# A streaming encoder layer on one core: part of the weights split ahead of the second phase, its first rows brought in piece by piece, and its first loads in another order

## The chip, the core and the metric

The kernel runs on one core of one Trainium2 chip. The time is the device time of one execution in microseconds (us); lower is better. A core has a matrix engine (TensorE, PE in the profile, with its weight loads as PEld), a vector engine (VectorE, DVE), an activation engine (ScalarE, ACT), GpSimd (POOL) and a sync engine (SyncE, SP) that here does nothing but issue DMA transfers. Each engine works through its own list of instructions in order; semaphores hold an instruction back until what it needs is there.

## What is computed

One layer of a hybrid streaming encoder over a prompt of 2048 tokens and a sample of 32 tokens (2080 columns together), model width 1024, float32 throughout:

```
h   = rmsnorm(x)
z   = h @ W_in          # 1024 -> 5376: q, k, v, four gates, conv input, two merge gates
A   : sliding-window attention, 8 heads on 2 kv heads, yA = (attn * silu(gA)) @ W_A
B   : gated causal convolution of width 3,             yB = (B * conv(C * u) * silu(gB)) @ W_B
r   = x + (sigmoid(mA) * yA + sigmoid(mB) * yB) @ W_o
out = r + sigmoid(r @ W_pg) * (p @ W_pp)
```

The keys, values and convolution rows that a next step needs are written out too.

## The kernel before

**Two halves of a float32.** TensorE multiplies in a rounded format (fp32r). To keep float32 accuracy, both operands are cut in two: `hi` is the rounded value (a copy on ACT), `lo = value - hi` the rest (a subtraction on DVE). Every product is then three matmuls, hi*hi, hi*lo and lo*hi. So each weight piece of 128x512 that comes from HBM costs one ACT copy and one DVE subtraction before TensorE can use it. The raw piece lies in one of 8 buffers tagged `wf`, the split piece in one of WB = 5 buffers of the pool `wp` (`w` in the profile); the split function is at L228, its two operations at L229 and L230.

**Fewer products by sums of quadrants.** The large products are done by a Strassen-like scheme: seven products p = 1 to 7 of quadrant combinations in place of eight. Of the weight operand, p = 1, 2 and 4 are plain quadrants, and p = 7, 5, 6 and 3 are sums of up to four quadrants (`WS`, L332).

**First phase (L1201 to L1230, first product at L611).** z = h @ W_in for all tokens, in groups g = 0 to 20 of output columns: first the token columns 0 to 1023 (steps named `(0, g, p)`), then the rest (`(1, g, p)`, and with a fourth element, a letter, where a second level of the scheme runs at L749). A hand-written list `steps` orders them. What comes out goes to DRAM: q, k, v, gates, the conv rows `z_y`, the tanh of the merge gates `z_t`. Beside this, after step `(0, g, 6)` for g = 1 to 8, `quad_sums` (L368) prepares the quadrant sums of W_o (UO) and W_pg (UPG) for the second phase: four raw loads of 256 KB on SP, four additions on DVE, four stores to the DRAM tiles `quad_sum` by GpSimd (L377). Its tiles come from the pool of 15 rows `tmp`. Near the end of the phase, after steps `(1, 20, 6)` and `(1, 20, 7)`, `conv_rows` (L855) loads and splits the first three of four token blocks of the conv rows (12 loads at L850, 12 splits at L233 and L234) that the second phase starts with.

**Second phase (all of it recorded at L158 of the profile).** Here the order of the instructions of every engine is written out by a planner in the kernel: it advances a clock of its own (`now`) by a modelled cost for every instruction (`cost_queue`, L119), keeps count of free buffers (`limit`, `live`), and emits each instruction when the model says that its inputs are there. Loads land 5.2 us after their issue in its model. TensorE's work is the list `plan` (L307): yB for the blocks 0 to 3, pp = p @ W_pp, yA of block 0 and 1, the 28 products of W_o and the 28 of W_pg for the first half of the tokens (`first`, `products_of`, L296), yA of block 2 and 3, and the 28 + 28 products of the second half. Between these, the attention of 17 token tiles is started at given points of TensorE's work (L2022): every 11 us for the first eight. An attention tile loads q (`zq`), k and v (`zkv`) and the rotary table (`cs`), transposes on TensorE and takes turns on ACT, DVE and GpSimd.

**Weights in the second phase.** `next_loads` (L1924) is called whenever nothing else is due. It first issues the row loads of the next units, then raw weight loads up to LOOK = 11 pieces ahead into the `wf` buffers, while SP is not more than 0.5 us booked, and then starts splits (`split_w`, L1910) in order as soon as one of the 5 `w` buffers is free. One product of W_o or W_pg uses one piece; so does one unit of yA.

```
while n_load[0] < min(len(worder), used[0] + LOOK) and busy["Y"] < now[0] + 0.5:
    ...
    if raw_key(key):
        uu, e = raw_key(key)
        eY.dma_start(out=t, in_=wu[uu, :, 4 * e:4 * e + 4, :])
    else:
        eY.dma_start(out=t, in_=quad_sum[key[2:4]][:, WS[key[4]]])
```

The functions that the change touches, with the line numbers of the profile:

## Time and profile before

| | |
|---|---|
| median of 3 runs | 1530.45 us (1529.68 to 1532.38) |
| the profiled execution | 1533.35 us |
| its span, first to last instruction | 1531.6 us |
| share of the span: ACT, GpSimd | 53%, 24% |
| moved by DMA | 346.89 MB, mean 226 GB/s |
| weight splits in the second phase (`w<-wr`, L158) | 168 on ACT, 168 on DVE |

In rows of stretches of time, an engine's busy time stands in us with the number of its instructions; PEclk is the clock that TensorE was granted (1.00 is full speed), and the DMA share is the mean busy share of the 16 DMA engines. A matmul's span in the trace overlaps with the next one's, so that "busy" for PE means that some matmul was under way; what is missing from the length of the stretch is time in which PE stood still. In rows of waits stand: the instruction that waited, what ended the wait, us in total, how often, the longest. In rows of groups: busy us and mean ns of one, then the idle time before. In rows of DMA issues: KB of one and the us from issue to landing.

### The profile page before, as it was taken

Reading aid. Unit: us, or ns where it says so; the run is one execution under the profiler, and the core shown is the slowest. Engines: PE = TensorE matmul, PEld = TensorE weight load, DVE = VectorE, ACT = ScalarE, POOL = GpSimd, SP = SyncE. Lnnn points to the kernel's source line nnn. Section 1 sums busy time; section 2 is a strip of 40 time slices with the busy share of each in tenths; the row PEclk is TensorE's granted clock in tenths of the full one; section 3 lists DMA queues with packets and bytes.
Section 4 is the critical chain, followed back from the end, with each engine's and each line's share of the span. In section 5 each row is a group of like instructions: output and inputs, shape, how many; then the busy total and the mean of one; then the engine's idle time right before and its main releaser. Section 6 shows DMA issues by size and latency. Waiting matters only on the chain.

```text
span 1531.6 us, 27944 instructions
## 1 busy us (share of the span) xinstructions
PE 1500.7 (98%) x9553; PEld 1355.8 (89%) x9553; DVE 1227.2 (80%) x2330; ACT 818.2 (53%) x1933; POOL 370.5 (24%) x534
## 2 busy tenths in 40 slices
PE   9999999999999999999999999999999999999998
PEld 7878888888889999999999889998877787999998
DVE  7896887875589776899965878868998899769777
ACT  8353354344467634434544546786766586544453
POOL 2133332332212222333222111103313213211201
PEclk9999999999999999999999999999999999999999
DMA  9479886898777845343556776658947749985959
GB/s 340 151 276 342 313 295 216 282 344 266 241 279 257 315 149 195 112 132 119 175 192 187 265 234 205 210 186 231 239 127 184 187 128 300 312 240 145 254 143 288
DMA packets 199231, 346.89 MB, mean 226 GB/s; under 512 B 23728, under 2 KB 57072, under 8 KB 199088
## 3 DMA queue, kind: packets, MB, share of 16 engines
q1 hardware_dynamic: 157008, 239.42, 48.4%
q0 software_dynamic: 32432, 87.85, 19.9%
q10 hardware_dynamic: 9648, 17.83, 3.1%
q8 instruction: 75, 1.23, 0.3%
q14 instruction: 68, 0.56, 0.1%
HBM read 227.66 MB, written 117.46 MB: 225 GB/s over the span
## 4 chain that ended last, share of the span: by engine, by line
PE 38%; DVE 7%; ACT 3%; DMA 2%; issue 2%; SPq 0%; ACTq 0%; DVEq 0%
PE b L158 17%; PE yB L158 5%; PE yA L158 5%; PE O L158 2%; PE S L158 2%; DVE c L158 1%; PE la L749 1%; PE pp L158 1%; PE a L611 1%; PE a L613 1%; PE a L616 1%; PE PT L158 1%; DVE w L158 1%; DVE xb_l L158 1%; DVE tk L158 1%
## 5 line engine op out<-in xcount | busy, mean ns | idle before, releaser
L158 PE MATMUL b<-xb_h,w 128*128 128x264 f32 (+1 forms) x1344 | 315.3, 326 | 7.2 <-DVE c L158 4.5
L158 PEld LDWEIGHTS b<-xb_h,w 128*128 128x128 f32 x1344 | 225.1, 190 | 27.6 <-DVE c L158 4.2
L613 PE MATMUL a<-x_l,w 128*128 128x264 f32 (+1 forms) x744 | 228.1, 320 | 0.0
L611 PE MATMUL a<-x_h,w 128*128 128x264 f32 (+1 forms) x744 | 227.1, 319 | 0.0
L158 PE MATMUL b<-xb_l,w 128*128 128x264 f32 (+1 forms) x672 | 218.4, 325 | 0.8 <-DVE xb_l L158 0.8
L616 PE MATMUL a<-x_h,w 128*128 128x264 f32 (+1 forms) x744 | 201.6, 320 | 0.0
L229 ACT CAST w<-wr 128x512 fp32r<-128x512 f32 (+1 forms) x180 | 110.2, 619 | 105.7 <-PE c L616 35.4
L230 DVE TENSOR_TENSOR w<-wr,w 128x512 fp32r<-128x512 f32 (+1 forms) x180 | 136.1, 767 | 33.9 <-ACT w L229 32.7
L158 ACT CAST w<-wr 128x512 fp32r<-128x512 f32 x168 | 103.5, 623 | 105.7 <-PE b L158 53.0
L611 PEld LDWEIGHTS a<-x_h,w 128*128 128x128 f32 x744 | 139.9, 188 | 10.5
L613 PEld LDWEIGHTS a<-x_l,w 128*128 128x128 f32 x744 | 139.7, 188 | 10.7
L158 PEld LDWEIGHTS b<-xb_l,w 128*128 128x128 f32 x672 | 127.8, 190 | 10.8 <-DVE xb_l L158 1.6
L616 PEld LDWEIGHTS a<-x_h,w 128*128 128x128 f32 x744 | 125.0, 188 | 10.7
L158 DVE TENSOR_TENSOR w<-wr,w 128x512 fp32r<-128x512 f32 x168 | 117.8, 706 | 14.1 <-ACT w L158 13.4
L749 PE MATMUL la<-x_h,w 128*128 128x264 f32 x516 | 112.2, 285 | 1.9 <-ACT w L229 1.2
L613 PE MATMUL c<-x_l,w 128*128 128x512 f32 (+1 forms) x336 | 110.7, 339 | 0.0
L611 PE MATMUL c<-x_h,w 128*128 128x512 f32 (+1 forms) x336 | 110.6, 340 | 0.0
L229 ACT CAST w<-a 128x512 fp32r<-128x512 f32 x82 | 49.7, 620 | 98.1 <-DVE a L360 31.5
L616 PE MATMUL c<-x_h,w 128*128 128x512 f32 (+1 forms) x336 | 100.4, 340 | 0.0
L810 DVE SCALAR_TENSOR_TENSOR u<-u,c 128x264 f32<-128x264 f32 (+1 forms) x125 | 59.4, 506 | 44.5 <-ACT u L805 30.0
L158 PE MATMUL yB<-ycs_h,w 128*128 128x264 f32 (+1 forms) x384 | 91.0, 326 | 0.0
L805 ACT COPY u<-a 128x264 f32<-128x264 f32 (+1 forms) x114 | 47.4, 437 | 80.7 <-PE a L616 80.7
(435 smaller groups left out, 3877.8 us busy)
## 6 DMA issues: line engine op xcount, KB each, us to landing
wr<-in_wu SPq DMA_DIRECT2D x177, 256.0 KB, 4.1
a<-in_wu SPq DMA_DIRECT2D x116, 256.0 KB, 5.3
wr<-ws SPq DMA_DIRECT2D x74, 256.0 KB, 3.5
wr<-qs SPq DMA_DIRECT2D x64, 256.0 KB, 3.9
ws<-a POOLq DMA_DIRECT2D x63, 256.0 KB, 4.0
qs<-a POOLq DMA_DIRECT2D x24, 256.0 KB, 5.8
z_s<-s2n POOLq DMA_DIRECT2D x21, 264.0 KB, 5.0
s<-z_s SPq DMA_DIRECT2D x21, 264.0 KB, 4.5
```

Source lines behind the costliest of these rows:

```text
L158: return f(**kw)
L229: nc.scalar.copy(out=hi, in_=src)
L230: nc.vector.tensor_tensor(out=lo, in0=src, in1=hi.bitcast(F32), op=sub)
L611: nc.tensor.matmul(out=ps[:, :cn], lhsT=w[:, 0, k], rhs=x[0][:, c0:c0 + cn], start=first and k == 0, stop=False, skip_group_check=True)
L613: nc.tensor.matmul(out=ps[:, :cn], lhsT=w[:, 0, k], rhs=x[1][:, c0:c0 + cn], start=False, stop=False, skip_group_check=True)
L616: nc.tensor.matmul(out=ps[:, :cn], lhsT=w[:, 1, k], rhs=x[0][:, c0:c0 + cn], start=False, stop=k == 3, skip_group_check=True)
L749: nc.tensor.matmul(out=ps[:, :m], lhsT=w[:, a, k], rhs=r[:, cols], start=q in "ABG" and j == 0 and e == 0, stop=j == 1 and e == 2, skip_gr ...
L805: nc.scalar.copy(out=t[:, c0:c0 + cn], in_=ps[:, :cn])
L810: nc.vector.scalar_tensor_tensor(out=t[:, c0:c0 + cn], in0=t[:, c0:c0 + cn], scalar=-1.0, in1=ps[:, :cn], op0=mul, op1=sub)
```

## The change

Six things are done at once.

1. For the 16 quadrant sums of W_o (p = 7, 5, 6, 3 for n = 0 to 3), `quad_sums` now also splits the sums, and stores hi and lo, 512 KB in place of 256 KB (`store_split`). The sums of W_pg are stored raw as before.
2. The 8 raw pieces of W_A, which yA uses (`piece_split`), are loaded in the first phase, split, and stored as hi and lo in `wa_split`.
3. In the second phase, pieces that are stored split (`stored`) skip the raw load and the split: one DMA of 512 KB goes straight into a `w` buffer when one is free. Each of the 8 pieces of W_A is used in each of four blocks, each of the 16 sums in two halves, which makes 64 such loads in place of 64 raw loads with their 64 ACT copies and 64 DVE subtractions.
4. The loads of the sums and pieces come at steps `(0, g, 6)`, their arithmetic at `(0, g, 7)`, a few products later; W_o at g = 1, 3, 5, 7, W_pg at g = 9, 11, 13, 15, the pieces of W_A at g = 2, 4, ... 16. Their tiles come from a pool of five of their own (`zpool`) and not from `tmp`.
5. The conv rows of blocks 0, 1 and 2 are loaded earlier than they are split: loads after the steps `(1, 20, 1)`, `(1, 20, 6)` and `(1, 19, 5)`, splits after `(1, 20, 6)`, `(1, 19, 5)`, and for block 2 one row at a time in the last set of products.
6. In the second phase, the second attention tile starts at 6 us of TensorE's work and not at 11, and no raw weight is loaded before the planner's clock has passed 8 us.

```diff
--- before.py
+++ after.py
@@ -363,18 +363,45 @@
         for p, i in WS.items():
             nc.gpsimd.dma_start(out=wsum[g][:, i], in_=sums[g][p])
 
-    quad_sum = {(x, n): dram.tile([P, 4, 4, P], F32, tag=f"qs{x}_{n}", name=f"qs{x}_{n}") for x in (UO, UPG) for n in range(4)}
+    quad_sum = {(x, n): dram.tile([P, 4, 1 + (x == UO), 4 * P], F32, tag=f"qs{x}_{n}", name=f"qs{x}_{n}")
+                for x in (UO, UPG) for n in range(4)}
+    wa_split = [dram.tile([P, 2, 4 * P], F32, tag=f"wa{n}", name=f"wa{n}") for n in range(8)]
+
+    def quad_load(name, u, e):
+        t = zp.tile([P, 4 * P], F32, tag="z", name=name)
+        nc.sync.dma_start(out=t.rearrange("p (a b) -> p a b", a=4), in_=wu[u, :, 4 * e:4 * e + 4, :])
+        return t
+
+    def store_split(dst, t, name):
+        h = tmp(f"h{name}", F32R)[:, :512]
+        split(h, t.bitcast(F32R), t)
+        nc.gpsimd.dma_start(out=dst[:, 0], in_=h.bitcast(F32))
+        nc.gpsimd.dma_start(out=dst[:, 1], in_=t)
 
     def quad_sums(x, n):
-        t = {}
-        for name, u, e in (("a11", n, 0), ("a21", n + 4, 0), ("a22", n + 4, 1), ("a12", n, 1)):
-            t[name] = tmp(f"{name}_{x}_{n}")[:, :512].rearrange("p (a b) -> p a b", a=4)
-            nc.sync.dma_start(out=t[name], in_=wu[x + u, :, 4 * e:4 * e + 4, :])
-        t["sc"] = tmp(f"sc_{x}_{n}")[:, :512].rearrange("p (a b) -> p a b", a=4)
+        t = {name: quad_load(f"{name}_{x}_{n}", x + u, e)
+             for name, u, e in (("a11", n, 0), ("a21", n + 4, 0), ("a22", n + 4, 1), ("a12", n, 1))}
+        yield
+        t["sc"] = zp.tile([P, 4 * P], F32, tag="z", name=f"sc_{x}_{n}")
         for o, v, w in (("sc", "a11", "a21"), ("a21", "a21", "a22"), ("a11", "a11", "a21"), ("a12", "a12", "a11")):
             nc.vector.tensor_tensor(out=t[o], in0=t[v], in1=t[w], op=add)
         for p, o in ((7, "sc"), (5, "a21"), (6, "a11"), (3, "a12")):
-            nc.gpsimd.dma_start(out=quad_sum[x, n][:, WS[p]], in_=t[o])
+            if x == UO:
+                store_split(quad_sum[x, n][:, WS[p]], t[o], f"{p}_{x}_{n}")
+            else:
+                nc.gpsimd.dma_start(out=quad_sum[x, n][:, WS[p], 0], in_=t[o])
+
+    def piece_split(n):
+        t = quad_load(f"wa_{n}", UY + n, 0)
+        yield
+        store_split(wa_split[n], t, f"wa_{n}")
+
+    def stored(key):
+        if key[0] == "q" and key[3] == 0:
+            return wa_split[key[2] - UY]
+        if key[0] == "B" and key[2] == UO and key[4] in WS:
+            return quad_sum[key[2:4]][:, WS[key[4]]]
+        return None
 
     def raw_key(key):
         if key[0] == "q":
@@ -852,12 +879,16 @@
 
     yc = {}
 
-    def conv_rows(b):
+    conv_in = {}
+
+    def conv_load(b):
+        conv_in.update({(b, c): load_row(f"yc{b}_{c}", z_y[c], b) for c in range(4)})
+
+    def conv_split(b, cs=range(4)):
         nt = blk(b)[1]
-        for c in range(4):
-            t = load_row(f"yc{b}_{c}", z_y[c], b)
+        for c in cs:
             yc[b, c] = pair(f"ycs{b}_{c}")
-            split_half(yc[b, c][0][:, :nt], yc[b, c][1][:, :nt], t[:, :nt])
+            split_half(yc[b, c][0][:, :nt], yc[b, c][1][:, :nt], conv_in.pop((b, c))[:, :nt])
 
 
 
@@ -1198,7 +1229,15 @@
         refills[at_step[at_]] = p
     after = {at_step[1, pairs_[9], 2, "C"]: sets[0]}
     after.update({at_step[1, sets[i - 1][-1], 5]: sets[i] for i in range(1, len(sets))})
-    sums_at = {(0, 1 + 2 * n + e, 6): (x, n) for n in range(4) for e, x in enumerate((UO, UPG))}
+    zpool = tc.tile_pool(name="zpool", bufs=5)
+    zp = zpool.__enter__()
+    sums_at = {(0, 1 + 2 * n, 6): quad_sums(UO, n) for n in range(4)}
+    sums_at.update({(0, 9 + 2 * n, 6): quad_sums(UPG, n) for n in range(4)})
+    sums_at.update({(0, 2 + 2 * n, 6): piece_split(n) for n in range(8)})
+    sums_at.update({(0, g, 7): v for (_, g, _), v in sums_at.items()})
+    conv_at = {(1, G - 1, 1): lambda: conv_load(0), (1, G - 1, 6): lambda: (conv_split(0), conv_load(1)),
+               (1, G - 2, 5): lambda: (conv_split(1), conv_load(2))}
+    conv_at.update({(1, sets[-1], 3 + c % 2, "DE"[c // 2]): lambda c=c: conv_split(2, (c,)) for c in range(4)})
     prep = [at_step[0, g, 7] for g in range(7, G)]
     for i, todo in enumerate(steps):
         if i < NS:
@@ -1206,15 +1245,12 @@
         if todo[0][:2] == (0, 0) and todo[0][2] in (3, 4):
             make_x(todo[0][2])
         run(todo)
-        if todo[0] == (1, G - 1, 6):
-            conv_rows(0)
-            conv_rows(1)
-        if todo[0] == (1, G - 1, 7):
-            conv_rows(2)
+        if todo[0] in conv_at:
+            conv_at[todo[0]]()
         if i in prep:
             next(X1, None)
         if todo[0] in sums_at:
-            quad_sums(*sums_at[todo[0]])
+            next(sums_at[todo[0]], None)
         if i in after:
             load_second_products(after[i])
         if i in refills:
@@ -1224,6 +1260,7 @@
             refill(refills[i])
     nc.gpsimd.dma_start(out=cpo, in_=halo)
     nc.gpsimd.dma_start(out=cso, in_=halo_out)
+    zpool.__exit__(None, None, None)
     xpool.__exit__(None, None, None)
 
 
@@ -1939,8 +1976,11 @@
             u["loaded"] = True
             load_at[0] += 1
 
-        while n_load[0] < min(len(worder), used[0] + LOOK) and busy["Y"] < now[0] + 0.5:
+        while n_load[0] < min(len(worder), used[0] + LOOK) and busy["Y"] < now[0] + 0.5 and now[0] > 8:
             i = n_load[0]
+            if stored(worder[i]) is not None:
+                n_load[0] += 1
+                continue
             fin[0] = 0.0
             if room["wf"] < 1:
                 break
@@ -1951,16 +1991,27 @@
                 uu, e = raw_key(key)
                 eY.dma_start(out=t, in_=wu[uu, :, 4 * e:4 * e + 4, :])
             else:
-                eY.dma_start(out=t, in_=quad_sum[key[2:4]][:, WS[key[4]]])
+                eY.dma_start(out=t, in_=quad_sum[key[2:4]][:, WS[key[4]], 0].rearrange("p (a b) -> p a b", a=4))
             raw_of[i] = t
             landed[i] = fin[0] + 0.5
             n_load[0] += 1
         while n_split[0] < len(worder) and room["w"] > 0:
             i = n_split[0]
-            if landed.get(i, 1e9) > now[0] or busy["S"] >= now[0] + (0.3 if i > used[0] + 2 else 1.5):
-                break
-            room["w"] -= 1
-            go(split_w(i))
+            src = stored(worder[i])
+            if src is not None:
+                if busy["Y"] >= now[0] + 0.5:
+                    break
+                room["w"] -= 1
+                w = wp.tile([P, 2, 4, P], F32R, tag="w", name=f"w{i}")
+                W2[i] = w[:, 0], w[:, 1]
+                fin[0] = 0.0
+                eY.dma_start(out=w.bitcast(F32).rearrange("p a b c -> p a (b c)"), in_=src)
+                w_ready[i] = fin[0] + 0.5
+            else:
+                if landed.get(i, 1e9) > now[0] or busy["S"] >= now[0] + (0.3 if i > used[0] + 2 else 1.5):
+                    break
+                room["w"] -= 1
+                go(split_w(i))
             n_split[0] += 1
 
     work = [0.0]
@@ -2019,7 +2070,7 @@
     e1, e2 = T[f"yA1_{NA[1][0]}"], T[f"yA2_{NA[2][0]}"]
     left.update({0: 4, 1: 4, 2: 5, 3: 5})
     for e in range(len(TILES)):
-        t = 11 * e if e < 8 else e1 - 30 + (e2 - e1) * (e - 8) / 9
+        t = (0, 6)[e] if e < 2 else 11 * e if e < 8 else e1 - 30 + (e2 - e1) * (e - 8) / 9
         begin.append((t, lambda e=e: go(attention(e), None, {"z": 1, "tmp": 2})))
     begin.append((T["yB0_6"], lambda: load_p(2)))
     begin.append((T["yB0_7"], lambda: load_p(3)))
```

## The prediction

> **What bounds the kernel now.** I read the page first, then a table by stage of the span, then what TensorE waited for, then the queue of SP around the worst place. The page says that TensorE is the bound:
>
> ```profile
> span 1531.6 us, 27944 instructions
> PE 1500.7 (98%) x9553; PEld 1355.8 (89%) x9553; DVE 1227.2 (80%) x2330; ACT 818.2 (53%) x1933; POOL 370.5 (24%) x534
> ```
>
> The change takes no matmul away, so it can win only what TensorE loses by standing still, and by the slower clock after it. The stretches of the span show where that is (columns: length, then busy us of PE, PEld, DVE, ACT, POOL, then granted clock, DMA share, GB/s):
>
> ```profile
> 100.00:440.00 340.00, 340.00 (x1469) 274.54 (x1468) 255.08 (x417) 141.47 (x268) 101.12 (x187) 1.00 0.84 294
> 840.00:900.00 60.00, 55.56 (x376) 51.70 (x376) 45.15 (x98) 27.81 (x67) 9.61 (x9) 0.97 0.79 268
> 900.00:1040.00 140.00, 138.16 (x997) 128.73 (x996) 107.88 (x247) 101.90 (x351) 18.98 (x16) 1.00 0.66 202
> 1040.00:1200.00 160.00, 154.13 (x807) 128.78 (x806) 148.51 (x286) 102.20 (x282) 46.03 (x50) 0.99 0.75 196
> 1200.00:1300.00 100.00, 92.69 (x466) 76.67 (x465) 90.55 (x176) 73.46 (x202) 18.98 (x19) 0.93 0.71 202
> 1300.00:1380.00 80.00, 80.00 (x630) 78.51 (x629) 59.56 (x112) 38.87 (x91) 16.37 (x19) 1.00 0.96 270
> 1380.00:1520.00 140.00, 140.00 (x1152) 140.00 (x1151) 113.81 (x214) 66.28 (x124) 21.59 (x25) 1.00 0.77 205
> ```
>
> Length less PE: 4.4 us idle at the seam of the phases (840 to 900), 1.8 to 1040, 5.9 to 1200, 7.3 to 1300, together 19.5. Length times (1 - clock): 1.8, 0, 1.6 and 7.0, together 10.4, a little of which falls on the idle time itself; I take 9. So 28.5 us is all that these stages can give back. From 100 to 440 and from 1300 to 1520 nothing stands still: there the change can only cost. Between 1040 and 1300 DVE is busy 91 to 93%. What TensorE waited for, over the whole span:
>
> ```profile
> PE b L158 <- DVE c L158: 4.5, 3, 3.3
> PE PT_s L158 <- ACT Ps L158: 3.2, 1, 3.2
> PE pq L158 <- DMA zq<-z_q: 3.2, 1, 3.2
> PE b L158 <- ACT xb_h L158: 2.8, 1, 2.8
> PE la L749 <- ACT w L229: 1.2, 1, 1.2
> ```
>
> Behind the waits of about 3 us the clock fell to half, behind the shortest, at 857, it did not (the last row has PE's columns alone):
>
> ```profile
> 884.00:886.00 2.00, 2.00 (x11) 2.00 (x10) 0.00 (x0) 0.53 (x2) 0.70 (x1) 0.50 1.03 397
> 1126.00:1128.00 2.00, 2.00 (x8) 1.81 (x8) 1.73 (x6) 2.00 (x8) 0.00 (x0) 0.50 0.61 77
> 1210.00:1212.00 2.00, 2.00 (x6) 1.61 (x6) 1.92 (x7) 1.25 (x4) 0.39 (x1) 0.50 0.00 0
> ...
> 858.00:860.00 2.00, 2.00 (x18) 1.00 0.49 115
> ```
>
> **The seam, 840 to 900.** SP's timeline shows eight conv rows issued in one go, then five raw weights that hold the queue for 7.4 us, and the second tile's q (`zq`) only after them, at 877.77; in the chain of waits it lands 5.40 us later, with TensorE idle since 880:
>
> ```profile
> 836.98 4.56 SPq L850 DMA_DIRECT2D yc<-z_y  x8
> 865.30 7.39 SPq L158 DMA_DIRECT2D wr<-in_wu  x5
> 877.77 0.42 SPq L158 DMA_DIRECT2D zq<-z_q  x1
> 877.77 5.40 DMA zq<-z_q
> ```
>
> Starting that tile 5 us sooner and raw weights after 8 us puts zq ahead of those five loads on SP, at about 866, so that it lands by 872 and this wait goes. The raw weights are moved behind it by some 8 us; five split pieces of yB, each used in four blocks, cover that, and nothing waits for it. The conv rows, loaded some products before they are split, no longer stop ACT in front of the last weight copies (`la` and `lc` wait for `w` there): that gives about 1.2, the last row of the waits. The work of the 12 splits stays; only its place moves. On SP their loads, 0.57 us each by the first row, now go ahead of a few of the phase's last raw weights; four at a time make 2.3 us, under the time that a split piece lies ready. Of 4.4 + 1.8 = 6.2 I take 5.5.
>
> **The 64 splits.** One costs 623 ns on ACT and 706 on DVE:
>
> ```profile
> L158 ACT CAST w<-wr 128x512 fp32r<-128x512 f32 x168 | 103.5, 623 | 105.7 <-PE b L158 53.0
> L158 DVE TENSOR_TENSOR w<-wr,w 128x512 fp32r<-128x512 f32 x168 | 117.8, 706 | 14.1 <-ACT w L158 13.4
> L158 DVE TENSOR_TENSOR w<-wr,w 128x512 fp32r<-128x512 f32 x42 | 32.0, 765 | 0.5 <-ACT w L158 0.2
> L158 DVE TENSOR_TENSOR w<-wr,w 128x512 fp32r<-128x512 f32 x24 | 17.3, 727 | 0.1
> ```
>
> So 64 x 0.623 = 39.9 us leave ACT and 64 x 0.706 = 45.2 leave DVE, but only those in stages that wait count. The third row is 1040 to 1200: of its 42 splits about 24 go (8 of yA of block 1, 16 of W_o), 24 x 0.765 = 18.4 us. DVE falls there from 148.5 to 130 us, and TensorE needs 154.1 - 1.6 = 152.5: DVE has slack of 22 us where it now has 4. Of 5.9 + 1.6 = 7.5 I take 6.0; what stays are chains through attention. The last row is 1200 to 1300, the products of W_pg, whose weights stay raw: only about 4 of 24 (the first of yA of block 2) go, 4 x 0.727 = 2.9. DVE then needs 87.6 us and TensorE 92.7 - 7.0 = 85.7. DVE remains the limit, so no more than 100 - 87.6 = 12.4 can come back; an engine that works in order and is that full leaves waits behind. It enters the stage less late, which may spare one of the two large waits; I take 4.0, between 0 and 12.4. From 900 to 1040 the 8 copies for yA of block 0 leave ACT (73% busy): half of 1.8, 0.9.
>
> The clock makes the steps uneven. The Trainium skill (TensorE: Matmul & The Clock Gate, Part 1) says that the clock is halved after an idle window of about 3.4 us that runs freely, so a wait merely cut to 1 or 2 us would give back its whole clock part too. The trace agrees: half clock behind waits of 2.8 to 3.3 us, 1.00 behind the 1.2 us one. By that rule alone 1200 to 1300 would give 7.0 rather than my 4.0, and the sum would end at 1514.0 rather than 1517.0; it is held by the case "all lags go" below and the range.
>
> **What the stored pieces cost.** Each is 512 KB, and its load waits for a free `w` buffer where a raw load had eight more buffers to run ahead. The cover is four pieces. In yA a piece is 24 matmuls, by this row of the chain 24 x 14.24 / 117 = 2.92 us, so 11.7 us:
>
> ```profile
> 1324.13 14.24 PE yA L158 x117
> ACT w L158 <- PE yA L158: 18.3, 10, 2.3
> SPq L158 <- DVE c L158: 38.4, 19, 5.8
> wr<-qs SPq DMA_DIRECT2D x64, 256.0 KB, 3.9
> wr<-in_wu SPq DMA_DIRECT2D x13, 256.0 KB, 6.9
> 1310.00:1340.00 30.00, 30.00 (x247) 29.82 (x246) 21.39 (x43) 14.26 (x33) 6.90 (x8) 1.00 1.08 305
> 500.00:520.00 20.00, 20.00 (x167) 20.00 (x166) 13.86 (x26) 11.78 (x26) 5.61 (x10) 1.00 1.03 380
> ```
>
> The second row (1310 to 1380) shows raw pieces ready long before a buffer was. The third (from 1380) is the worst that SP stood before a store whose data were late, 5.8 us, with everything behind it. 256 KB land in 3.9 us as a rule and in 6.9 in the crowded stretch 1310 to 1380. For 512 KB the bounds are 3.9 us (nothing more for the second half) and 13.8 (twice the crowded row); I take 8, a crowded landing and a little, as the second half needs no second start. With 0.9 for release and issue this is 9 of 11.7 us: covered, unless it meets a long SP wait. In 1310 to 1340 the DMA share is 1.08 already, and 8 x 256 KB more in 30 us are 70 GB/s on top of 305: 375, against 380 in the busy stretch from 500, at the edge. I take 2 us lost in all of 1040 to 1465, bounds 0 and 15.
>
> A rule speaks against it here: the Trainium skill (DMA: Bandwidth & Descriptors, Specifications) gives about 358 GB/s of HBM for a core. By it, yA of block 2 would last 30 x 375 / 358 = 31.4 us, an estimate, and the sum would end at 1518.4. The trace disagrees, with 380 GB/s over 20 us and 397 in the row at 884.
>
> **The first phase.** 8 raw loads, 16 more stores for W_o and 16 for W_A, 40 x 256 KB = 10.5 MB, join the 294 GB/s x 340 us = 100 MB of 100 to 440, at a DMA share of 0.84: 0.93. The 24 splits add 24 x 0.706 = 17 us to DVE's 255 of 340 and 15 to ACT's 141. The sums of W_pg move back into the stretch in which the second half of x is prepared:
>
> ```profile
> 190.00:330.00 140.00, 140.00 (x607) 113.00 (x606) 112.77 (x182) 61.14 (x127) 41.41 (x75) 1.00 0.79 276
> ```
>
> with their 16 additions and some six splits DVE has about 22 x 0.7 = 15 us more there, 128 of 140. Each split waits for its copy on ACT, and DVE's following weight splits stand behind it; each store queues on GpSimd, 101 of 340 busy, ahead of stores only. TensorE shows no idle time in this stage and the weights run ahead, which hides it; if that cover fails in a crowded slice, it costs a few us. I take 1, bounds 0 and 6. The upper one is a third of the added 17 us of DVE.
>
> **Sum.** -5.5 - 0.9 - 6.0 - 4.0 + 2 + 1 = -13.4. The profiled execution took 1533.35 us (its span 1531.6 and 1.75 around it), which makes 1519.95; the median of the runs shown is 1530.45, 2.9 less, so I forecast 1517.0.
>
> **Rivals.** *All lags go.* The waits after 1200 are an inheritance of the crowded stage ahead: then DVE's 87.6 us are the only floor. Gains 6.2 + 1.8 + 7.5 + 12.4 = 27.9, less up to 3: about 1505. For it: 1206 and 1272 are single long waits, not many small ones; against: DVE is at 91% there with work that stays. *Gains taken back.* Only the seam (5.5) and half of the 6.9 to 1200 (3.5) come, nothing after 1200, and new DMA waits take 5: -4, 1526, with 1523 to 1533 around it. For it: the DMA share of 1.08. It also covers the case that the framework, which orders the first phase, leaves the conv rows where they were (1.2 less). *The stored pieces come too late.* With five buffers, a piece whose buffer takes L us from release to landing sets a period of (L + 2.92) / 5. It decides from L = 11.7; at 17 (6 us of SP standing, 11 to land) the period is 3.98 instead of 2.92, and the 32 stored units from 1311 to 1465 lose 32 x 1.06 = 34 us, against 15.4 of gains by the sum above (16.4 less 1 of the first phase): 1549. No change would be at L = 14.1, 32 x 0.48 = 15.4 us. For it: the 5.8 us stand and the upper bound of 13.8 us; against: the rows are the worst of each kind and would have to hold for most pieces.
>
> **How the numbers follow.** A measurement of this kernel can tell about 0.2%, 3.1 us. Forecast (1510 to 1523) 0.56; all lags go 0.18; taken back 0.15; too late 0.11. The middle of "taken back" lies just under 1527.4 and more of its spread above: 0.06 of its 0.15 go to faster, 0.09 to the same. So faster 0.56 + 0.18 + 0.06 = 0.80, same 0.09, slower 0.11. The range 1505 to 1530 leaves out the late case and some ends, 2 in 10.
>
> **What would show it.** Right: `w<-wr` at L158 with 104 instead of 168 on each engine; no wait of `pq` for `zq`; clock 1.00 from 880 to 890; idle time in the stage of W_o's products down from 5.9 to under 2, and DVE at most 85% there; some 3 us idle left in W_pg's; 346.89 MB grown by 104 x 0.262 = 27.3. Wrong: TensorE waiting for a DMA into `w` for more than 3 us in all, PE idle in the first phase between 100 and 440, or the stage of W_pg as slow as before.

## The result and the profile after

The changed kernel takes 1541.26 us (median of 4 runs, 1539.13 to 1546.06), the kernel before 1530.6 beside it: ratio 1.0073, 95% interval 1.0046 to 1.0099. It is slower by 0.7%, where 1517.0 and a range of 1505 to 1530 were forecast. The profiled execution took 1542.36 us, 9.0 more than that of before. First the page of the changed kernel: TensorE is busy as before, DVE and ACT lost the work that they were to lose, and the span grew.

```profile
span 1540.6 us, 27844 instructions
...
PE 1501.9 (97%) x9553; PEld 1354.6 (88%) x9553; DVE 1196.2 (78%) x2290; ACT 795.0 (52%) x1893; POOL 388.5 (25%) x566
```

The same stretches as before, in the same columns:

```profile
100.00:440.00 340.00, 328.77 (x1398) 264.32 (x1397) 252.53 (x411) 144.24 (x276) 113.98 (x215) 0.98 0.87 306
840.00:900.00 60.00, 59.34 (x444) 56.82 (x443) 43.04 (x90) 32.23 (x69) 13.55 (x14) 1.00 0.74 245
900.00:1040.00 140.00, 138.32 (x1004) 129.38 (x1003) 108.88 (x252) 94.70 (x331) 19.92 (x16) 1.00 0.71 221
1040.00:1200.00 160.00, 158.85 (x865) 134.01 (x865) 135.37 (x274) 98.05 (x289) 46.12 (x48) 1.00 0.88 243
1200.00:1300.00 100.00, 95.36 (x494) 78.59 (x493) 93.09 (x180) 72.24 (x201) 21.54 (x21) 0.98 0.74 204
1300.00:1380.00 80.00, 73.55 (x540) 70.53 (x539) 39.94 (x79) 25.93 (x63) 15.53 (x18) 0.96 1.04 312
1380.00:1520.00 140.00, 139.65 (x1146) 139.44 (x1145) 105.50 (x198) 57.51 (x110) 21.97 (x26) 1.00 0.85 238
```

The first row had no idle time before; now TensorE stands for 11.2 of its 340 us. From the seam to the stage of W_pg (rows 2 to 5) it stands for 0.7 + 1.7 + 1.1 + 4.6 = 8.1 us, where it was 19.5, about as forecast. (In the changed kernel the second phase starts 17 us later and its first yA 10 us later, so rows 2 to 4 hold work that lay that much earlier before.) Then the row from 1300, which had none, has 6.5 us and a clock of 0.96. TensorE's waits say what stands there:

```profile
PE a L638 <- ACT u L832: 6.1, 2, 3.7
PE yA L158 <- DMA w<-wa: 5.9, 2, 4.8
PE b L638 <- ACT w L229: 3.7, 1, 3.7
PE pr L158 <- DVE sq L158: 3.5, 2, 1.9
PE b L158 <- DVE xb_l L158: 2.3, 5, 0.7
PE pq L158 <- DMA zq<-z_q: 2.0, 1, 2.0
```

Rows 1 and 3 lie between 280 and 360 in the first phase, row 2 between 1300 and 1340: TensorE waits for a 512 KB piece of W_A. The waits of before at 880 (for `zq`) and ahead of 1126 are gone; the last row is another tile's, between 1200 and 1300. The groups and the DMA issues show that the change does what it says, 104 splits and 64 loads of 512 KB:

```profile
L158 ACT CAST w<-wr 128x512 fp32r<-128x512 f32 x104 | 63.7, 620 | 92.9 <-PE b L158 50.5 <-PE yA L158 23.0 <-PE 2_0_610 L158 9.4
...
L158 DVE TENSOR_TENSOR w<-wr,w 128x512 fp32r<-128x512 f32 x104 | 72.1, 699 | 12.6 <-ACT w L158 11.7 <-DMA w<-wa 0.3
...
w<-wa SPq DMA_DIRECT2D x32, 512.0 KB, 5.7
w<-qs SPq DMA_DIRECT2D x32, 512.0 KB, 5.4
```

For all kernels below, the span is cut at four instants that every one of them has: the first matmul of yB (its operand is a conv row), the first and last matmuls of yA (its operand is a merged attention row), and the first yA of block 2. They are read off the rows of these matmuls in each kernel's profiled execution; the columns are differences in us, the last two the medians and ratios of the timed runs. The kernel before ran beside each on the same chip, with medians from 1528.4 to 1530.6, so the ratio is what compares. A single profiled execution lies up to 3.4 us from the median of its kernel (that of before 2.8 above), so small differences in the columns count for little.

| kernel | to first yB | to first yA | to yA of block 2 | to end of yA | rest | median us | ratio to before (95%) |
|---|---|---|---|---|---|---|---|
| before | 857.6 | 164.0 | 289.8 | 67.8 | 152.4 | 1530.6 | |
| after | 874.5 | 156.9 | 281.0 | 75.0 | 153.2 | 1541.26 | 1.0073 (1.0046 to 1.0099) |
| e1: items 5, 6 alone | 854.1 | 158.4 | 285.3 | 67.6 | 152.5 | 1520.78 | 0.9950 (0.9933 to 0.9966) |
| e2: second phase alone | 856.2 | 157.0 | 280.2 | 75.2 | 152.5 | 1524.7 | 0.9971 (0.9958 to 0.9984) |
| e3: other pool | 867.9 | 157.8 | 280.3 | 75.0 | 152.4 | 1535.62 | 1.0048 (1.0033 to 1.0063) |
| e4: no split arithmetic | 865.5 | 157.0 | 280.1 | 75.3 | 152.4 | 1533.03 | 1.0028 (1.0013 to 1.0044) |
| e5: e3, W_pg earlier | 862.7 | 157.0 | 280.7 | 75.8 | 152.5 | 1530.53 | 1.0013 (1.0001 to 1.0026) |
| e6: e3, W_A partly raw | 869.9 | 156.9 | 279.6 | 74.7 | 152.5 | 1531.98 | 1.0016 (1.0004 to 1.0028) |
| e7: e3, W_A raw, W_pg earlier | 860.6 | 158.3 | 279.6 | 74.0 | 152.5 | 1524.43 | 0.9972 (0.9961 to 0.9983) |
| e8: e3 and e4 | 861.8 | 157.0 | 279.7 | 75.6 | 152.4 | 1530.83 | 1.0012 (1.0001 to 1.0024) |
| e9: item 5 alone | 855.0 | 163.5 | 287.2 | 67.6 | 152.4 | 1527.47 | 0.9988 (0.9973 to 1.0004) |
| e10: item 6 alone | 854.4 | 159.0 | 287.2 | 67.6 | 152.4 | 1523.35 | 0.9960 (0.9942 to 0.9978) |
| e11: e7, less traffic | 860.6 | 158.8 | 279.5 | 66.7 | 152.7 | 1519.39 | 0.9928 (0.9904 to 0.9951) |
| e12: e7, tiles spread | 860.3 | 158.4 | 265.5 | 81.6 | 152.8 | 1519.94 | 0.9929 (0.9907 to 0.9951) |
| e13: e1, tiles spread | 855.9 | 158.3 | 271.9 | 85.0 | 152.7 | 1525.66 | 0.9979 (0.9964 to 0.9993) |
| e14: after, tiles spread | 874.4 | 156.9 | 267.9 | 79.5 | 152.8 | 1532.43 | 1.0022 (1.0009 to 1.0034) |
| e15: e7, no split arithmetic | 860.7 | 158.3 | 280.2 | 72.8 | 152.7 | 1527.37 | 0.9990 (0.9978 to 1.0001) |
| e16: e12, sums late | 879.7 | 159.9 | 266.5 | 81.7 | 153.5 | 1541.61 | 1.0078 (1.0057 to 1.0100) |
| e17: all late, tiles spread | 889.4 | 157.1 | 268.7 | 78.4 | 153.3 | 1548.17 | 1.0121 (1.0099 to 1.0143) |
| e18: e12, W_pg later | 863.5 | 158.8 | 266.1 | 81.5 | 152.7 | 1526.22 | 0.9986 (0.9970 to 1.0002) |

Before, e1, e2, e9, e10 and e13 do the same work up to the conv rows, and their first column reads 854.1 to 857.6: a difference under 3.5 us in it says nothing by itself. After less before, column by column, is +16.9, -7.1, -8.8, +7.2 and +0.8, together the 9.0 us of the spans.

### The profile page after: what moved, and what is told of

It is laid out like the page before. It is cut to its first block, busy times and chain, and to the rows that moved or that the text cites. A ratio compares the mean times of both kernels' runs of the same rounds, so it can differ in the third digit from the quotient of the medians.

```text
span 1540.6 us, 27844 instructions
## 1 busy us (share of the span) xinstructions
PE 1501.9 (97%) x9553; PEld 1354.6 (88%) x9553; DVE 1196.2 (78%) x2290; ACT 795.0 (52%) x1893; POOL 388.5 (25%) x566
## 2 busy tenths in 40 slices
DMA packets 202941, 374.14 MB, mean 243 GB/s; under 512 B 24368, under 2 KB 57712, under 8 KB 202800
## 4 chain that ended last, share of the span: by engine, by line
PE 72%; DMA 11%; DVE 7%; issue 6%; ACT 3%; POOL 1%; SPq 0%; POOLq 0%; DVEq 0%; ACTq 0%
PE b L158 13%; PE a L638 7%; PE a L643 7%; PE a L640 7%; PE yB L158 6%; PE la L776 5%; PE yA L158 4%; PE c L638 3%; PE c L640 3%; PE c L643 3%; DMA wr<-in_wu 3%; PE lc L776 2%; DVE c L158 2%; PE O L158 2%; PE S L158 1%
## 5 line engine op out<-in xcount | busy, mean ns | idle before, releaser
L158 PE MATMUL b<-xb_h,w 128*128 128x264 f32 (+1 forms) x1344 | 311.5, 324 | 0.0
L158 ACT CAST w<-wr 128x512 fp32r<-128x512 f32 x104 | 63.7, 620 | 92.9 <-PE b L158 50.5
L158 PE MATMUL yA<-ac_h,w 128*128 128x264 f32 (+1 forms) x384 | 93.6, 330 | 6.0 <-DMA w<-wa 5.9
L776 PEld LDWEIGHTS la<-x_h,w 128*128 128x128 f32 x516 | 86.9, 188 | 1.6 <-ACT w L229 1.0
```

What stands on the lines that cost most here:

```text
L158: return f(**kw)
L776: nc.tensor.matmul(out=ps[:, :m], lhsT=w[:, a, k], rhs=r[:, cols], start=q in "ABG" and j == 0 and e == 0, stop=j == 1 and e == 2, skip_gr ...
```

## The experiments

**The halves of the change, e1 and e2.** e1 takes items 5 and 6 alone, e2 the second phase of the change with the first phase's work of before (one piece of W_A is split and stored, and all 64 loads read it, so the products are of other weights).

```diff
+ e1: before, conv_at / conv_load / conv_split, (0, 6)[e], now[0] > 8
- e2: return wa_split[key[2] - UY], return quad_sum[key[2:4]][:, WS[key[4]]]     (stored)
+ e2: return wa_split[0]     (both)
+ e2: quad_sums and sums_at of before, piece_split(0) after step (0, 10, 6)
```

> The kernel before with the fifth and sixth point of the change alone (conv rows loaded ahead and split piece by piece, second attention tile at 6, raw weights after 8); no piece is stored split. Theory: the seam is independent of the stored pieces, the wait for zq and the one for the last weight copies go, worth 4 to 6 us: about 1525.5. Rival: the seam's gain needs the relief of ACT and DVE by the stored pieces, and the loads only change places: within 1.5 us of the kernel before.

> The second phase of the changed kernel with the first phase's work of the kernel before: the sums are made and stored raw at the old steps from the old pool, one single piece is split and stored, and all 64 split loads of the second phase read that one piece (so the weights of these products are wrong; the number and size of the loads are those of the change). Theory: the 9 to 10 us that the change loses are 17 us lost in the first phase less 8 won in the second, so this takes about 1522, with the first yB at 858. Rival: the first phase's end moved for the conv rows or the scheduler's order and not for the extra work: 1535 or more, first yB after 868. The long wait in yA of block 2 should be there in both.

The seam by itself is worth 1528.48 - 1520.78 = 7.7 us, more than the 4 to 6 expected. With the first phase of before, the change's second phase beats before by only 0.3%, and not e1: what it wins up to yA of block 2 (285.3 to 280.2) it loses from there (67.6 to 75.2). And the first phase, not the second, is what makes the change slower.

**The first phase: pool and arithmetic, e3, e4, e8.** In the changed kernel SP stands before loads into the pool of five, until earlier sums are stored or added. The waits of SP and DVE from 250 to 345, SP's timeline and two stretches:

```profile
SPq L372 <- DMA qs<-a: 8.0, 4, 4.4
SPq L372 <- DVE a L387: 4.5, 2, 3.7
```

```profile
DVE b L544 <- DMA b<-in_xT: 8.4, 5, 5.0
```

```profile
266.28 5.16 SPq L372 DMA_DIRECT2D a<-in_wu  x2
...
328.51 4.85 SPq L372 DMA_DIRECT2D a<-in_wu  x3
```

```profile
20.00:60.00 40.00, 37.99 (x162) 29.97 (x161) 31.60 (x54) 22.46 (x43) 8.66 (x15) 0.96 0.78 288
280.00:340.00 60.00, 49.11 (x198) 38.69 (x199) 49.04 (x79) 18.10 (x32) 22.54 (x43) 0.94 0.87 306
```

SP's longest wait in that stretch is another, 48.0 us for free buffers of raw weights, but the kernel before has it too (67.4). Behind 5.16 and 4.85 us of standing queue the weights and rows of x, of the same queue, come late; DVE stands for x (second fence; 2.3 us in the same stretch before), and TensorE loses 10.9 of 60 us from 280, with clock 0.94. How this reaches TensorE is seen in two places, rows of the chain of work from 262 to 284 and a wait between 318 and 340:

```profile
274.53 8.10 DMA wr<-in_wu
...
282.73 0.63 ACT w L229
...
283.40 0.80 PE b L638
```

```profile
ACT w L229 <- DVE a L360: 7.4, 1, 7.4
```

A raw weight that SP issued at 274.53 lands 8.10 us later, and TensorE starts again behind its copy. At 337.6 a weight copy on ACT has waited 7.4 us for a sum on DVE, which had stood 3.1 us for x ahead of it; behind that copy in ACT's order comes the copy `u` for which TensorE waits. At 20 to 60 it is the other way round: the five buffers are free from the start, so that four loads of the first sums and one of W_A went out from 27 to 38 us, among the first weights, and TensorE loses 2.0 of 40, with clock 0.96.

```diff
- e3: t = zp.tile([P, 4 * P], F32, tag="z", name=name)
+ e3: t = tmp(name)[:, :512]
- e4: split(h, t.bitcast(F32R), t)         (store_split; the sum is stored twice as it is)
```

> The changed kernel with the tiles of the sums and pieces from the pool of 15 rows in place of the five buffers of their own. Theory of the buffers: five buffers make SP stand until the stores of the sums before have landed, and being free from the start they let the first five loads slip ahead of the first weights; without them the first phase loses 5 us or less of its 17: about 1529. Rival, the amount of work (10.5 MB more of DMA and 24 splits): the loss stays, 1538 to 1542.

> The changed kernel without the 24 copies and 24 subtractions in the first phase: the sums and pieces are stored twice as they are (these weights are then wrong), with all loads and stores in place. Theory of the buffers and queues: nearly all of the loss stays, 1537 to 1541. Rival, the arithmetic that stands in line on ACT and DVE: the loss of the first phase goes by half or more, 1532 or less.

> As the kernel with the pool of 15 rows, and without the 24 copies and subtractions in the first phase (stored twice as they are; these weights are wrong). Theory: of the 16.9 us of the first phase the five buffers made 6.6 and the splits standing in line most of the rest, so that the first yB starts at 856 to 859 and the time is about 1524.5. Rival, the 10.5 MB more of transfers: first yB at 863 or later, 1530 or more.

The pool costs 6.6 us (874.5 to 867.9), the arithmetic of the splits 9.0 with the small pool and 6.1 with the large one. Neither explains all: with both out (e8, between its two cases) 861.8 - 857.6 = 4.2 us are left. In e3 the loss from 20 to 60 is gone, and that from 280 falls from 10.9 to 4.9. SP waits 23 us at L372 from 0 to 440, where it waited 57; but from 250 to 345 it waits there no less (16.6 and 15.7), now for rows of `tmp` that the preparation of x holds. So the 6.6 us of the pool are shown; which of its waits make them is not.

**What is moved where, e5, e6, e7, e15.**

```diff
- e3: sums_at (0, 9 + 2 * n, 6): quad_sums(UPG, n), (0, 2 + 2 * n, 6): piece_split(n)
+ e5: sums_at (0, 2 + 2 * n, 6): quad_sums(UPG, n), (0, 9 + n, 6): piece_split(n)
+ e6: e3, stored(): W_A only for key[1] < 2
+ e7: e5 without piece_split, W_A raw
- e15: e7 without split(h, t.bitcast(F32R), t)
```

> As the kernel with the pool of 15 rows (first yB at 867.9, 1535.6 us), but W_pg's sums back at g = 2, 4, 6 and 8 as before the change, and the pieces of W_A at g = 9 to 16, one each. Theory of the place: the stalls between 280 and 360 come from W_pg's loads and sums moved into the stretch in which the second half of x is prepared; with them out of it the first yB starts at 857 to 861, and the time is 1525 to 1529. Rival, the split arithmetic wherever it stands: first yB after 864, 1532 or more.

> As the kernel with the pool of 15 rows, but W_A is loaded stored-split only for blocks 0 and 1; for blocks 2 and 3 it comes raw and is split as before the change. Theory of the late landing: yA of blocks 2 and 3 with the products between them takes 67.7 us again instead of 75.0, and the time is 7 us under that kernel's 1535.6, about 1528.5. Rival: the transfers there are crowded anyway because the stage before ended sooner and leaves its stores to this one: 73 us or more.

> As the kernel with the pool of 15 rows, without the pieces of W_A (raw in all four blocks, as before the change) and with W_pg's sums back at g = 2, 4, 6 and 8; W_o's sums are stored split. Theory: the sums of W_o carry the relief of the crowded stages (yA of block 0 to yA of block 2 in 280 to 282 us, where the kernel with the seam alone takes 285.3 and the changed one 281.0), the first phase ends as in the kernel before (first yB 855 to 859) and yA of block 2 to 3 takes 67.7: 1517 to 1520. Rival: the relief came from W_A's pieces: 284 us or more; or the 16 splits at g = 1 to 7 cost the first phase 4 us or more.

> The run with W_o's sums alone stored as halves (1524.4 us, first yB at 860.6) without the 16 copies and 16 subtractions of the split; the sum is stored twice as it is, so that W_o's hi is not rounded and its lo is the sum itself. If the split arithmetic, in line on ACT and DVE, is what is left of the first phase's loss: first yB at 854 to 856 (the seam run: 854.1), time 1518 to 1520. Rival, the earlier loads and doubled stores are: 859 to 861, time 1523 to 1525.

W_pg's sums among the preparation of x, where e5 has single pieces of W_A instead, cost 5.2 us (867.9 to 862.7, between e5's two cases), those pieces some 2 more (860.6). With both out, the split arithmetic costs nothing (860.7 against 860.6): it was dear only together with the rest of the work. What is still lost then lies in what e15 keeps, the earlier loads and the doubled stores of W_o's sums, as its rival had it. e6 and e7 show the second thing. With W_A raw, TensorE no longer waits for `w<-wa`, and the stretch from yA of block 2 is as long as with stored pieces (74.7 and 74.0). The waits and the chain of e7 there:

```profile
PE b L158 <- DVE xb_l L158: 5.1, 2, 3.3
```

```profile
1303.00 19.58 PE yA L158 x162
1322.58 6.74 DMA tk<-z_t
```

TensorE now waits behind another load, that of the merge gates (`tk`), in place of a weight's.

**The two parts of the seam, e9 and e10.**

```diff
+ e9:  before with conv_at / conv_load / conv_split
+ e10: before with (0, 6)[e] and now[0] > 8
```

> The kernel before with item 5 alone (conv rows loaded and split piece by piece). The seam in whole (items 5 and 6) took 7.7 us of the median: first phase 3.5, from the first yB to the first yA 5.6 (at the seam run's 158.4), the stages of W_o and W_pg 4.5, less what is given back. If the two items have a place each, as my prediction put it: here the first phase ends 2 to 4 us sooner, the stretch from first yB to first yA stays at 164 or loses what was won, since the second tile's q still comes behind the raw weights; time 1525 to 1530. Rival, one of them alone does it all, because the second phase only inherits how late its rows come: then this kernel has 158 to 160 us there, too, and a time near 1521.

> The kernel before with item 6 alone (second attention tile at 6 us, raw weights after 8 us of the planner's clock). If the two items have a place each: the first phase stays at 857 to 858 us, the stretch from first yB to first yA falls from 164.0 to 158 to 160, no wait of the second tile for its q; time 1523 to 1526. Rival, as in the run beside it: the rows of the conv input are what matters, here nothing changes by more than 2 us, 1529 to 1532.

SP's timeline of e9 and then of e10, and between them TensorE's wait in e9:

```profile
874.52 0.42 SPq L158 DMA_DIRECT2D zq<-z_q  x1
```

```profile
PE pq L158 <- DMA zq<-z_q: 3.4, 1, 3.4
```

```profile
868.37 1.19 SPq L158 DMA_DIRECT2D zq<-z_q  x1
```

The order of the loads sends q some 6 us sooner and takes the 3.4 us wait away: 164.0 to 159.0 up to the first yA. The conv rows piece by piece can't be told from no change (0.9973 to 1.0004).

**What takes the relief back, e11 to e14.** e11 takes traffic away: the accumulating load of r at the end of W_pg's products is left out for the first half, so that half of the output misses r. e12 to e14 start the second half's attention tiles over 20 us more (`e1` and `e2` in the lines of the code are two times of the planner, not runs).

```diff
- e11: if "rs" not in u:
+ e11: if "rs" not in u and s:
- e12 (on e7), e13 (on e1), e14 (on after): e1 - 30 + (e2 - e1) * (e - 8) / 9
+ e12, e13, e14:                            e1 - 30 + (e2 - e1 + 20) * (e - 8) / 9
```

> The run with sums of W_o stored as halves, W_A raw, tiles from tmp, W_pg's sums early (1524.4 us), with the accumulating load of r at the end of W_pg's products left out for the first half of the tokens: 16 DMAs of 256 KB less, 4.2 MB, so that the first half of the output misses r. Theory: the stretch from yA of block 2 on loses its 6 to 7 us since the transfers from 1260 to 1335 fill the queues (DMA share 1.02 to 1.09, 22.5 MB in 75 us) and a shorter stage ahead of them only moves the wait; 3.7 MB less in that window are 12 us of transfers, so the stretch falls from 74.0 to 67 to 69 us and the time to 1517 to 1519. Rival: the chain over DVE and ACT (merge of the gates) is what is late, whatever the transfers: the stretch stays at 73 or more, time 1523 to 1525.

> The same run (1524.4 us) complete, with the attention tiles of the second half started over a stretch 20 us longer, so that some of their transfers and of their work on DVE falls behind the crowded stretch and into yA of blocks 2 and 3, where DVE is only half busy. If transfers crowd the end of W_pg's stage: from yA of block 2 on 74.0 falls to 68 to 71, and the time to 1518 to 1521. Rival: the tiles are not what crowds (most of the transfers there are the output, r, weights and merge gates), and later tiles only put the merge of block 3 at risk: 73 to 77 us there, 1524 to 1529.

> The kernel before with items 5 and 6 and the attention tiles of the second half started over a stretch 20 us longer; every weight is split as before. If the removal of splits is what makes the crowded stages shorter and the spread only keeps it from being given back: from the first yA of block 0 to the end of block 3's yA 351 to 353 us (352.9 without the spread, 347.1 with spread and W_o's sums stored split), time 1519 to 1521. Rival, the spread alone relieves the stage of W_pg, since it takes attention work out of it: 345 to 348, and with the seam run's first phase a time of 1513 to 1516, the best of all, and the stored pieces are worth nothing.

> The change as it is with the attention tiles of the second half started over a stretch 20 us longer. If transfers crowded around yA of block 2 take back the relief, as in the run with raw W_A: the stretch from the first yA of block 0 to the end of yA of block 3 falls from 356.0 to 347 to 350, time 1532 to 1536, the first phase still at 873 to 875. Rival, here the 512 KB pieces of W_A are late by themselves, whatever else is moved: 354 to 357, time 1539 to 1542.

The stretch 1260 to 1340 of e7 and then of e11:

```profile
1260.00:1340.00 80.00, 74.94 (x477) 67.69 (x476) 60.63 (x115) 46.92 (x113) 18.00 (x21) 0.96 1.05 299
```

```profile
1260.00:1340.00 80.00, 79.97 (x535) 73.12 (x535) 65.83 (x122) 51.27 (x123) 5.95 (x7) 1.00 0.84 265
```

With the DMA share down from 1.05 to 0.84, TensorE's idle time there goes, and from yA of block 2 to the end of yA it is 66.7 us, as short as before the change. The other loads land sooner, as these rows of the same stretch show, e7 and then e11:

```profile
wr<-in_wu SPq DMA_DIRECT2D x22, 256.0 KB, 8.2
```

```profile
wr<-in_wu SPq DMA_DIRECT2D x24, 256.0 KB, 4.3
```

So crowded queues took the relief back, as far as this run can tell: the loads left out also took 12 us of work from GpSimd (18.0 to 5.95) and let the output be stored sooner, and no run separates these from the transfers. The tiles started later shift the first yA of block 2, so only the sum of the third and fourth columns compares: 353.6 in e7, 347.1 in e12; 356.0 in after, 347.4 in e14, as its theory had it. In e13, with every split in place, the spread makes it worse, 356.9 against 352.9, which neither theory had; its waits name tiles late on DVE:

```profile
PE O L158 <- DVE ptl L158: 3.3, 5, 2.0
PE S L158 <- DVE qs L158: 2.8, 2, 1.8
```

So taking away W_o's splits is worth 356.9 - 347.1 = 9.8 us, but only with the tiles spread (without, 353.6 in e7 against 352.9 in e1); W_A's splits add nothing to it (347.4). Against e1, the better kernel with every split in place, 5.8 us are left.

**Is there a place that costs nothing? e16, e17, e18.** 100 to 200 us in e15 and in e13, where the first phase is that of before:

```profile
100.00:200.00 100.00, 96.14 (x408) 77.21 (x407) 75.22 (x121) 34.12 (x63) 40.21 (x76) 0.98 0.94 347
```

```profile
100.00:200.00 100.00, 100.00 (x432) 80.86 (x432) 78.18 (x126) 39.23 (x77) 34.90 (x66) 1.00 0.93 334
```

The queues were at 0.93 there before anything was added, so the sums were moved to where they have room.

```diff
- e12: sums_at by (0, g, 6), W_o at g = 1, 3, 5, 7, W_pg at 2, 4, 6, 8
+ e16: the eight sums over the steps (1, g, p), 500 to 780 us
+ e17: with the eight pieces of W_A too, and W_A stored
+ e18: e12 with W_pg at g = 16, 17, 18, 19
```

> The run with the tiles spread and W_o's sums alone stored as halves (1519.9 us; first yB at 860.3, then 158.4, 347.1 and 152.8), with the quadrant sums of both W_o and W_pg made in the second half of the tokens of the first phase, spread evenly from about 500 to 780 us, where the DMA share is 0.39 to 0.59 and TensorE has no idle time. If the place is what costs: first yB at 854 to 857, the rest unchanged, time 1513.5 to 1517, the best of all. Rival, the work costs wherever it lies, since DVE and ACT take it in line in front of weight splits (DVE is 95% busy from 700 to 750): 859 to 863 or later, time 1519 to 1524.

> All of the change's work (sums of W_o stored as halves, the eight pieces of W_A as halves, sums of W_pg), tiles from tmp, made in the second half of the tokens, and the attention tiles spread as in the run beside it. If place alone made the first phase late in the change: first yB at 855 to 858 instead of 874.5, then 156.9, 347 to 349 and 152.8, time 1514 to 1517. Rival, the amount is too much anywhere: 862 or later, time 1521 or more.

> The run with the tiles spread and W_o's sums alone stored as halves (1519.9 us, first yB at 860.3) with W_pg's four sums moved from 115 to 227 us to 360 to 430 us, where DVE is busy 58 to 70% and the DMA share is 0.73 to 0.93; W_o's stay at 97 to 215. If it takes room on both DVE and the DMA queues: the 4 us lost at 160 to 200 go, first yB at 854 to 857, time 1514 to 1517, the best of all. Rival, work put into the list costs wherever it lies, as at 440 to 850: 860 or later, time 1519 to 1525.

The theory, that a place with room costs nothing, fell in all three. Stretches and a wait of e16, then of e18:

```profile
440.00:520.00 80.00, 72.94 (x529) 69.40 (x528) 70.84 (x148) 55.23 (x122) 17.60 (x31) 0.96 0.84 288
600.00:700.00 100.00, 93.76 (x753) 93.34 (x752) 88.95 (x163) 40.16 (x88) 40.59 (x62) 0.97 0.59 187
```

```profile
PE a L636 <- ACT u L830: 6.2, 2, 5.5
```

```profile
160.00:200.00 40.00, 40.00 (x174) 32.33 (x173) 34.23 (x55) 19.65 (x44) 12.75 (x25) 1.00 0.84 286
400.00:440.00 40.00, 34.96 (x147) 27.74 (x146) 28.11 (x54) 14.65 (x26) 12.85 (x24) 0.94 0.95 327
```

```profile
PE la L774 <- ACT x_h L229: 4.7, 1, 4.7
```

In e16 TensorE loses 7.1 us from 440 to 520 (1.9 before). From 600 the DMA share is 0.59, and still 6.2 us go, in waits for a copy that empties TensorE's banks, with DVE at 89%. In e18 the loss at 160 to 200 is gone (40 of 40 us), and 5.0 us are lost at 400 to 440 instead, where the copies of the next half's x come late. Each place has some work of the phase that has no slack. A place without a price was not found, and what exactly stands in line in each was not followed to the end. The fastest kernels with a complete output are e12 and e1, 1519.94 and 1520.78; the intervals of their ratios overlap.

## Why the prediction was wrong

**The first phase: the step that failed.** "I take 1, bounds 0 and 6"; it is 16.9. On one path of runs: 6.6 the pool (after to e3), 5.2 the place of W_pg's sums (to e5), 2.1 W_A's pieces (to e7), and 3.0 that are left against before. The 2.1 lie within the spread of the column. The 3.0 do not: four kernels with the first phase of e7 or e15 read 860.3 to 860.7, six with that of before 854.1 to 857.6, and TensorE stands for 3.9 us from 100 to 200 in e15, for none in e13. The working summed busy shares (DVE 128 of 140, DMA 0.93) and found room. Neither is what broke: measured, both are lower (111 of 140 from 190 to 330, 0.87 from 100 to 440), and DVE was not full from 280 to 340 (49.04 of 60), it stood. The pool of five, which the prediction names nowhere in its sum, holds SP's queue until a store has landed, and behind that stand all loads of the phase. "The weights run ahead, which hides it" was the cover on which the 1 us rested; that cover comes through the very queue that stood. The size of each part is measured; the way from SP's standing to TensorE's is read off the waits above, and for e3 and the later places it was not followed. Two of the text's own signs of being wrong came, TensorE idle between 100 and 440 and more than 3 us of waiting for a DMA into `w` (5.9), beside its signs for the second phase (104 splits, 374.14 - 346.89 = 27.25 MB more).

**The seam: right**, -5.5 - 0.9 forecast, -7.1 up to the first yA. The mechanism, zq ahead of five raw loads, is shown by e10; the 1.2 us put down to the conv rows are not: e9 does not show them, and `la` waits for `w` in it for 1.0 (1.2 before).

**W_o and W_pg: right in size, in part by luck**, -6.0 - 4.0 forecast, -8.8 measured to yA of block 2. But e1, which takes no split away, has 285.3 there, -4.5, and e9 and e10 have -2.6. So the splits that are gone account for 4.3 us in the changed kernel and for 5.7 in e7, about half of the forecast; how much of the rest is the seam and how much the spread of one execution is open. DVE fell from 148.5 to 135.4, not to 130 (to 138.5 in 1050 to 1210, as far behind the first yA as the row of before), and the stage of W_pg still has 93.1 busy and 4.6 idle.

**The clock.** The prediction finds the trace in agreement with the window that it cites, and expects a wait cut to 1 or 2 us to cost no clock. Its three waits of 2.8 to 3.3 us are all shorter than that window, and in the changed kernel a wait of 2.0 us that ended at 1202.8 (`pq` for `zq`) is followed by half clock, one of 2.4 us that ended at 313.6 by full clock:

```profile
1204.00:1206.00 2.00, 2.00 (x6) 0.50 1.11 247
```

```profile
314.00:316.00 2.00, 2.00 (x10) 1.00 1.01 361
```

So in this case the length of the wait alone does not decide it, and a wait of 2 us can still cost clock.

**The new waits: mis-sized**, 2 forecast with bounds 0 and 15, 7.2 measured. A load of 512 KB was taken at 8 us; in the crowded stretch it takes 10.0, and 14.09 where it stands in the chain, with the queues full:

```profile
w<-wa SPq DMA_DIRECT2D x8, 512.0 KB, 10.0
```

```profile
1306.42 14.09 DMA w<-wa
```

```profile
1310.00:1340.00 30.00, 24.04 (x170) 23.18 (x169) 9.56 (x21) 4.23 (x8) 6.07 (x7) 0.89 1.07 333
```

The 375 GB/s that were to fit "at the edge" were not moved there: 333 at a share of 1.07, while TensorE stood for 6.0 of 30 us. The Trainium skill (DMA: Bandwidth & Descriptors, Specifications) gives about 358 GB/s of HBM for a core; here the trace stayed below it. That does not make 358 the limit that was met: e12 moved 408 GB/s over 20 us (120 to 140) at a share of 1.04. But the pieces are only the form of the loss: with raw W_A the stretch is as long (e6, e7), in e7 with a wait behind `tk`, and with less traffic the loss is gone (e11).

**The rivals.** "The stored pieces come too late" has the right sign and, for the most part, the wrong reason: by its period 32 units lose 34 us, while TensorE waited 5.9 us for W_A and lost 0.35 in 1380 to 1520. "Gains taken back" comes closest in the second phase (e2: 0.9971 of before). No rival had the first phase as its place: in the text every case that ended slower lay behind 1300, and that is why 0.80 stood on faster.

Sum: of the miss in the spans, 9.0 + 13.4 = 22.4 us, 15.9 are the first phase, 5.2 the new waits, 1.2 W_o and W_pg, 0.8 the rest, less 0.7 at the seam.

## What to carry to other kernels

Work that is moved ahead into a phase that shows no idle time has to be priced by who stands in line behind each of its instructions, queue by queue, and by when its buffers come free; busy shares under 1 are no cover, and moving it about found another wait in each place. Relief of a crowded stage is given back where the next stage has its own limit: here the transfers at the end of W_pg, and taking away work paid only together with spreading what else starts there. Where a change bundles parts, the cheapest one (an order of loads, e10: 0.4%) may hold most of the gain (e1: 0.5%, e12: 0.7%).

## What the runs showed of the hardware

A DMA of 512 KB landed in 5.4 to 5.7 us as a rule and in 10.0 (median of 8) between 1285 and 1345 of the changed kernel at a DMA share of 1.06, where 256 KB of raw weights took 10.0 as well (median of 5): there the size did not set the landing time. That the full queues did is likely, as the same 256 KB land in 8.2 us in e7 and 4.3 in e11. At a share above 1 the engines moved 305 GB/s (before, 1310 to 1340), 333 (the changed kernel, same stretch) and 408 (e12, 120 to 140), so a full share does not say how much is moved.
